# Stores moved from ScalarE's queue to GpSimd's queue with the one-packet option, and middle tiles computed in two rows

## The chip, the cores and the metric

The kernel runs on one core of a Trainium2 chip. The metric is the device time of one execution in microseconds, as the median of several runs. The span of a profile is about 1.4 us shorter than the device time of the same execution, so spans are compared with spans and times with times.

## The reference

```python
# x: 8192 x 8192 float32
def reference(x):
    a, b = np.split(x, 2, axis=-1)
    return a * (1 / (1 + np.exp(-b)))
```

It is a gated linear unit: the left half of each row times the sigmoid of the right half. 268.44 MB are read and 134.22 MB are written.

## The kernel before

The 8192 rows are cut into 32 tiles of 256 rows. A partition holds two neighbouring rows of x, so a load moves 128 pieces of 64 KB and a store 128 pieces of 32 KB. I call such a piece a "row" of the transfer; the records of the profile show one packet for each. Each of the 16 DMA engines has 8 rows of each transfer. There are two input slots and two output slots.

```python
    for i in range(n_tiles):
        # ... (bookkeeping of waits)
        load = nc.sync.dma_start(out=xs[i % SLOTS], in_=x_t[i])
        # ...
        if 0 < i < n_tiles - 1:
            parts = [(slice(0, R), slice(0, half))]
        else:                      # first and last tile: four quarters
            w = half // 2
            parts = [
                (slice(r, r + 1), slice(c * w, (c + 1) * w)) for r in range(R) for c in range(2)
            ]
        def store(cols):
            ins = nc.scalar.dma_start(out=out_t[i, :, cols], in_=os[i % SLOTS][:, cols])
            now["stores"].append(ins)

        for k, (r, c) in enumerate(parts):
            b = rows[:, r, 1, c]
            sig = nc.scalar.activation(out=b, in_=b, func=SIG)
            mul = nc.vector.tensor_mul(out=packed[:, r, c], in0=rows[:, r, 0, c], in1=b)
            # ... (which waits are kept: on odd tiles the sigmoid, else the product,
            #      waits for the store of two tiles before)
            if i == n_tiles - 1 and k > 0:
                store(chunks[k - 1])          # the last tile is stored in quarters
        store(chunks[-1] if i == n_tiles - 1 else slice(0, R * half))
```

## Time and profile before

| | before |
|---|---|
| time, median of 3 runs | 933.28 us (933.08 to 933.77) |
| span of the profile | 931.7 us |
| bytes, mean rate | 402.67 MB, 432 GB/s |
| VectorE (DVE), ScalarE (ACT), GpSimd (POOL) busy | 30%, 24%, 0% |
| period of a tile, (885.93 - 73.65) / 28 from the starts of the sigmoids of tiles 2 and 30 | 29.01 us |

The table says to look at the DMA engines and at nothing else: the compute engines idle most of the time, and the rate hardly leaves room. The prediction shows the lines. Two more carry the argument, the issues of the page (what, queue, how many, KB each, median us from issue to landing):

```profile
out_dram<-o_sb ACTq DMA_DIRECT2D x31, 4096.0 KB, 34.7
...
x_sb<-in_x_dram SPq DMA_DIRECT2D x32, 42.2
```

A store of 4 MB would take 9.7 us alone at 434 GB/s. It takes 34.7 us because it shares the engines with a load.

### The profile page before, as it was taken

Reading aid. Unit: us, or ns where it says so; the run is one execution under the profiler, and the core shown is the slowest. Engines: PE = TensorE matmul, PEld = TensorE weight load, DVE = VectorE, ACT = ScalarE, POOL = GpSimd, SP = SyncE. Lnnn points to the kernel's source line nnn. Section 1 sums busy time; section 2 is a strip of 40 time slices with the busy share of each in tenths; the row PEclk is TensorE's granted clock in tenths of the full one; section 3 lists DMA queues with packets and bytes.
Section 4 is the critical chain, followed back from the end, with each engine's and each line's share of the span. In section 5 each row is a group of like instructions: output and inputs, shape, how many; then the busy total and the mean of one; then the engine's idle time right before and its main releaser. Section 6 shows DMA issues by size and latency. Waiting matters only on the chain.

```text
span 931.7 us, 247 instructions
## 1 busy us (share of the span) xinstructions
DVE 278.7 (30%) x38; ACT 227.1 (24%) x39; POOL 0.2 (0%) x4
## 2 busy tenths in 40 slices
DVE  0333213333133331233312333123331233312333
ACT  1323330233311333113331133311333113332033
POOL 0000000000000000000000000000000000000000
DMA  9999999999999999999999999999999999999999
GB/s 405 428 450 428 422 456 405 450 428 428 450 418 438 428 436 442 428 428 450 447 408 428 442 459 428 413 460 411 450 428 425 453 408 447 428 428 450 425 430 405
DMA packets 9649, 402.67 MB, mean 432 GB/s; under 512 B 1072, under 2 KB 1072, under 8 KB 1072
## 3 DMA queue, kind: packets, MB, share of 16 engines
q1 hardware_dynamic: 4608, 268.44, 66.6%
q10 hardware_dynamic: 5040, 134.22, 33.4%
q14 instruction: 1, 0.01, 0.0%
HBM read 268.44 MB, written 134.22 MB: 432 GB/s over the span
## 4 chain that ended last, share of the span: by engine, by line
DMA 73%; DVE 15%; ACT 12%; issue 0%; ACTq 0%
DMA x_sb<-in_x_dram 73%; DVE o_sb L69 15%; ACT x_sb L68 12%; ACTq L62 0%; ACTq L68 0%
## 5 line engine op out<-in xcount | busy, mean ns | idle before, releaser
L69 DVE TENSOR_TENSOR o_sb<-x_sb 128x8192 f32<-128x8192 f32 (+1 forms) x38 | 278.7, 7344 | 647.1 <-ACT x_sb L68 647.1
L68 ACT ACTIVATE x_sb<-x_sb 128x8192 f32<-128x8192 f32 (+1 forms) x38 | 225.8, 5952 | 695.6 <-DMA x_sb<-in_x_dram 694.4
L68 ACT ACT_TABLE_LOAD x1 | 1.3, 1283 | 0.8 <-PEq L188 0.8
L188 POOL MEMSET const-bfloat16-1.0<- 128x1 bf16 x1 | 0.1, 102 | 0.0
L188 POOL MEMSET const-uint8-127<- 128x1 uint8 x1 | 0.1, 102 | 0.0
L188 POOL MEMSET const-float32-0.0<- 128x1 f32 x1 | 0.1, 99 | 0.2 <-issue 0.2
L188 POOL MEMSET const-float32-1.0<- 128x1 f32 x1 | 0.1, 99 | 0.0
## 6 DMA issues: line engine op xcount, KB each, us to landing
out_dram<-o_sb ACTq DMA_DIRECT2D x31, 4096.0 KB, 34.7
out_dram<-o_sb ACTq DMA_DIRECT2D x4, 1024.0 KB, 5.6
x_sb<-in_x_dram SPq DMA_DIRECT2D x32, 42.2
```

The costliest lines, as they stand in the source:

```text
L68: sig = nc.scalar.activation(out=b, in_=b, func=SIG)
L69: mul = nc.vector.tensor_mul(out=packed[:, r, c], in0=rows[:, r, 0, c], in1=b)
L188: nc = _bacc.Bacc("TRN2", target_bir_lowering=False, num_devices=1)
```

## The change

The intent is to take the stores off ScalarE's queue, to give each store to the DMA engines as one packet, so that it goes through in one piece, and to end a tile's product earlier by computing it in two rows (the two rows of x that a partition holds, not rows of a transfer).

```diff
         if 0 < i < n_tiles - 1:
-            parts = [(slice(0, R), slice(0, half))]
+            parts = [(slice(r, r + 1), slice(0, half)) for r in range(R)]
         ...
         def store(cols):
-            ins = nc.scalar.dma_start(out=out_t[i, :, cols], in_=os[i % SLOTS][:, cols])
+            to, of = out_t[i, :, cols], os[i % SLOTS][:, cols]
+            if i < n_tiles - 1:
+                ins = nc.gpsimd.dma_start(out=to, in_=of, single_packet=True)
+            else:
+                ins = nc.scalar.dma_start(out=to, in_=of)
             now["stores"].append(ins)
         ...
-            by_sigmoid = i % 2 == 1 and len(parts) == 1
-            implied(mul, *(s for s in old["stores"] if by_sigmoid or s not in freed))
-            if by_sigmoid:
-                for s in freed:
-                    tc.add_manual_dep(sig.ins, s.ins.name, DEP, reason="frees the output slot")
+            implied(mul, *(s for s in old["stores"] if k > 0 or s not in freed))
```

More of the change, by code (lines that the diff above doesn't have):

```diff
@@ L20, in _tiles @@
     P = nc.NUM_PARTITIONS
-    DEP = mybir.DependencyInfo(mybir.DependencyClass.Sync, mybir.DependencyReason.DATA)
     fp32 = mybir.dt.float32
```

## The prediction

> **What bounds the kernel now.** I read the page of the slowest core first, its engine shares, then its DMA rows and queues, then a table of stretches, then the waits of the load queue, and last the order of events at the end.
>
> ```profile
> span 931.7 us, 247 instructions
> DVE 278.7 (30%) x38; ACT 227.1 (24%) x39; POOL 0.2 (0%) x4
> ...
> DMA packets 9649, 402.67 MB, mean 432 GB/s; under 512 B 1072, under 2 KB 1072, under 8 KB 1072
> ...
> q1 hardware_dynamic: 4608, 268.44, 66.6%
> q10 hardware_dynamic: 5040, 134.22, 33.4%
> ```
>
> The busiest compute engine works 30% of the span. The 16 DMA engines are busy for 66.6 + 33.4 = 100% of it. 402.67 MB is no more than one read of x (8192 x 8192 x 4 = 268.44 MB) and one write of the result (134.22 MB). So no bytes can be saved, and the change saves none.
>
> The table of stretches says that this holds in each stage (columns: stretch, its length, busy time of DVE, ACT and POOL, clock, DMA share, GB/s):
>
> ```profile
> 100.00:158.00 58.00, 17.39 (x2) 14.06 (x2) 0.00 (x0) 1.00 1.00 434
> 842.00:900.00 58.00, 17.41 (x3) 14.06 (x2) 0.00 (x0) 1.00 1.00 434
> 914.00:918.00 4.00, 1.35 (x1) 3.29 (x2) 0.00 (x0) 1.00 1.01 434
> 918.00:922.00 4.00, 3.84 (x3) 2.77 (x3) 0.00 (x0) 1.00 0.86 371
> 922.00:926.00 4.00, 3.80 (x2) 1.48 (x1) 0.00 (x0) 1.00 1.01 426
> ```
>
> Two tiles (25.17 MB) take 58.0 us, that is 29.0 us a tile at 434 GB/s, and it is 434 with loads and stores mixed as well as with stores alone (914 to 918, after the last load). The one weak stretch is 918 to 922: 0.14 of 4 us, about 0.5 us. From the list of issues, a load takes 42.2 us from issue to landing and a store of 4 MB takes 34.7 us, both longer than the 29.0 us period, so each queue always has a transfer waiting behind the running one. The chain that ended last reads "DMA 73%; DVE 15%; ACT 12%", which looks as if 27% of compute could be gained. That is a trap: the chain follows one slot of two, and while it stands on ACT and DVE the DMA engines move the other slot's bytes. The load queue's own waits (859.9 us for the product, 30 times) are of the same kind: time in which the earlier load is still running.
>
> The end of the timeline (start, duration, engine, what):
>
> ```profile
> 885.93 7.03 ACT L68 ACTIVATE x_sb<-x_sb 128x8192 f32<-128x8192 f32 x1 [22.00 <-DMA x_sb<-in_x_dram]
> 892.99 8.69 DVE L69 TENSOR_TENSOR o_sb<-x_sb 128x8192 f32<-128x8192 f32 x1 [20.34 <-ACT x_sb L68]
> 901.72 0.34 ACTq L62 DMA_DIRECT2D out_dram<-o_sb  x1
> 914.71 3.71 ACT L68 ACTIVATE x_sb<-x_sb 128x2048 f32<-128x2048 f32 x2 [21.75 <-DMA x_sb<-in_x_dram]
> 916.65 4.49 DVE L69 TENSOR_TENSOR o_sb<-x_sb 128x2048 f32<-128x2048 f32 x2 [14.97 <-ACT x_sb L68]
> 918.98 0.34 ACTq L62 DMA_DIRECT2D out_dram<-o_sb  x1
> ```
>
> The last load lands at 914.7, and the first quarter of the last tile is issued as a store only at 919.0. Yet the DMA moves 434 GB/s between: the store of tile 30, issued at 901.7, is still being served. The old stores fill the hole in which the last tile is computed.
>
> **What the Trainium skill says.** "DMA: Bandwidth & Descriptors", section "Where 436 GB/s comes from", gives the ceiling as 16 ports x 32 B x 850 MHz = 435.2 GB/s. The trace agrees: 434 in the steady stages. An estimate from that page's figure: 402.65 MB cannot take under 925.2 us, 0.7% below the span. A gain of 2% would need 914.6 us and is excluded as long as the ceiling holds.
>
> The same page, section "Queues, rings and completion order", says that each DMA engine goes round its queues packet by packet and changes only between packets. The trace agrees: load 1 runs alone until the first store is issued at 32.82. With data from about 21.3, and some 1.6 us from issue to data (below), it has run 13.1 us of the 19.3 us that 8.39 MB take at 434 GB/s. Its other 6.2 us of work end near 44.2 (its sigmoid starts at 44.80), that is in 9.8 us, a share of 63%. Load rows here are 64 KB (268.44 MB / 4096 data packets), store rows 32 KB; turns of one row each give the load 2/3.
>
> The same page's "Specifications" give first byte about 1 us for GpSimd's path and 0.6 us for the other; no record of the kernel before shows GpSimd's path. "SBUF — State Buffer", section "Who interferes with whom", says that a product with two SBUF inputs takes GpSimd's read interface and not its write interface; the trace has no GpSimd work to check this.
>
> **The change, part by part.**
>
> Two rows. From the rows by shape: sigmoid 128x2048 1.903 us, 128x8192 7.031 us, so 128x4096 is about 3.61 us by a straight line; product 2.288 and 8.692 us, so about 4.42 us. The chain from landing to the end of the product goes from 7.03 + 8.69 = 15.7 us to 3.61 + 2 x 4.42 = 12.5 us. It frees the slot 3.2 us sooner, 30 times, 97 us if these lay on the path. But the next load is issued behind one that still has 29.0 - 12.5 = 16.5 us to run, where it had 13.2. Value in the steady state: 0. Busy time rises by 30 x (0.19 + 0.15) = 10 us on two engines that idle 70%: 0.
>
> The waits. Products wait for the store of two tiles before; it landed 34.7 us after an issue that lies 58 us back, so this wait was and stays empty: 0.
>
> The queue. 31 issues of 0.36 us leave ACT, off the path: 0. GpSimd, idle until now, builds the descriptors; I allow 2 us from the product to the first byte, and no queue runs dry by it: 0.
>
> The one-packet option. I take it, as an assumption, that each DMA engine's share of a store (8 rows of 32 KB, 256 KB) then is one turn. At 434/16 = 27.1 GB/s the turn takes 9.7 us, in which the load stands still; between two load rows (2.4 us each) the whole store goes by. The sum over a period stays 19.3 + 9.7 = 29.0 us, so the steady state stays. But a store lands 2 + up to 2.4 + 9.7 + about 1 = 13 to 15 us after issue, and a load takes 58.0 - 12.5 = 45.5 us. And at the end the order changes. Store 30 is issued 12.5 us after load 30 lands, starts by 12.5 + 2 + 2.4 = 16.9 and is out by 26.6 us, while load 31 ends at 29. So store 30 is wholly served ahead of load 31, and nothing is left to fill the hole.
>
> How large is this? In the kernel before, stores got 1/3 of 433.9 GB/s from about 34.4 to 914.1: 127.2 MB. The first 31 stores are 130.0 MB. So 2.8 MB, 6.5 us, were left behind the last load. A second way: in the window 918 to 922 the 32 KB packets end at about 920.4, and 920.4 - 914.1 = 6.3 us. These come before load 31 now: it lands at 914.7 + 6.4 = 921.1. From there the tail is not shorter. The first quarter's store is issued 918.98 - 914.71 = 4.27 us after landing and its 8 KB packets began near 920.7, 1.7 us later; its data starts 6.0 us after landing as before, four quarters need 4.19 MB / 434 = 9.7 us, and the rest is completion. Landing to end was 931.7 - 914.7 = 17.0 us and stays 16.7 to 17. Sum: 0 + 0 + 0 + 6.4 - 0.2 = +6.2 us, so 933.3 + 6.2 = 939.5 us.
>
> **The rivals.**
>
> A. The option does not make one turn of a store (the packet is cut, or a store waits for the load row after next and slips past the end of load 31). For it: there is no packet of that size in the trace, and the margin for store 30 is 29 - 26.6 = about 2.4 us. Against: the name. Then the turns are as before, some stores are left behind the last load, and the time is 933 to 934.5 us.
>
> B. GpSimd's path costs DMA rate: descriptors are fetched from memory, engines leave step, or the change between a long write turn and reads costs something each time. For it: nothing before shows this queue. Against: only 9 descriptors a tile and engine, and pure stretches of loads and of stores ran at 426 to 434 GB/s. 1% is 9 us: 942 to 950.
>
> C. The earlier product or the end of turn-taking lifts the rate, as reads and writes no longer mix. For it: 434 to 435.2 is open. Against: that is 0.3%, 2.5 us; with the tail lost or kept, 931 to 937.
>
> **Range and chances.** I give 0.65 to the full loss of the filler (938 to 940.5), 0.2 to A, 0.1 to B, 0.05 to C. The middle of this is near 938.5; 8 in 10 lie between 932.5 and 942. Faster by over 2% needs the ceiling broken: 0.01. Slower by over 2% needs 18.7 us, B at double strength: 0.03. Within 2%: 0.96.
>
> **What would show it.** Right: stores land in 13 to 15 us instead of 34.7 and loads in about 45.5; the period stays 29.0 us and the share of DMA 1.00 in the middle; the last load lands near 921; then a stretch of about 6 us with hardly any bytes; landing to end about 17 us. Wrong: stores still near 35 us and a last landing near 914.7 (A); a period over 29.2 us (B) or under 28.95 (C); or a hole of 6 us somewhere in the middle, which would mean that a load was issued too late.

## The result, and the profile after

The changed kernel takes 933.91 us (median of 4 runs, 933.23 to 934.19); the kernel before took 933.24 us beside it. The ratio is 1.0005 with a 95% interval of 0.9991 to 1.0019, so no difference is seen. A ratio is the mean time of one kernel's runs over that of the other's of the same rounds, so it is not quite the ratio of the medians quoted. Executions over 1.5% slower than the fastest of the same kernel are left out of the means.

The page of the changed kernel:

```profile
span 931.9 us, 316 instructions
DVE 280.8 (30%) x68; ACT 229.8 (25%) x69; POOL 16.8 (2%) x35
...
q1 hardware_dynamic: 4608, 268.44, 66.6%
q0 software_dynamic: 4464, 130.03, 32.3%
q10 hardware_dynamic: 576, 4.19, 1.1%
...
out_dram<-o_sb POOLq DMA_DIRECT2D x31, 4096.0 KB, 37.9
...
x_sb<-in_x_dram SPq DMA_DIRECT2D x32, 45.5
```

(q1 carries the loads, q0 the stores that GpSimd issues, q10 those that ScalarE issues.) The move did happen: 130.03 MB now go by the software queue q0. But its 4464 records are 31 x 144, that is 128 rows and 16 semaphore writes a store, as on the old queue. And a store does not land in 13 to 15 us, as the prediction has it. It lands in 37.9 us. That is 34.7 + 3.2 us: the product ends 3.2 us earlier, the store is issued 3.2 us earlier, and it lands when it did before. The load shows the same shift, from 42.2 to 45.5 us.

Two tiles in the middle and the stretches at the end (the same columns as in the prediction):

```profile
842.00:900.00 58.00, 17.52 (x4) 14.24 (x4) 1.06 (x2) 1.00 1.00 434
914.00:918.00 4.00, 1.20 (x1) 3.14 (x2) 0.00 (x0) 1.00 0.95 410
918.00:922.00 4.00, 3.81 (x3) 2.48 (x2) 0.00 (x0) 1.00 0.88 377
922.00:926.00 4.00, 3.68 (x2) 1.91 (x1) 0.00 (x0) 1.00 1.01 428
```

The 6 us without bytes that the prediction expected near the end are not there. The end of the timeline:

```profile
885.92 7.12 ACT L71 ACTIVATE x_sb<-x_sb 128x4096 f32<-128x4096 f32 x2 [21.72 <-DMA x_sb<-in_x_dram]
889.57 8.76 DVE L72 TENSOR_TENSOR o_sb<-x_sb 128x4096 f32<-128x4096 f32 x2 [20.08 <-ACT x_sb L71]
898.62 0.53 POOL L63 DMA_DIRECT2D out_dram<-o_sb  x1 [28.30 <-DVE o_sb L72]
914.86 3.71 ACT L71 ACTIVATE x_sb<-x_sb 128x2048 f32<-128x2048 f32 x2 [21.82 <-DMA x_sb<-in_x_dram]
```

Sigmoid, product and issue of tile 30 come as predicted, 12.7 us after the landing at 885.92. The last load lands at 914.86 us, not at 921, and the bytes of earlier stores that are still to move after it are the same: counted from some 0.6 us before the last tile's sigmoid, when the data of load 31 are through, to the end, the queues of stores move 6.88 MB before (from 914.1 us) and 6.84 MB after (from 914.3 us: 4.19 on q10 and 2.65 on q0). Less the 4.19 MB of the last tile this is 2.69 and 2.65 MB. I call it the filler. The prediction needed it to be zero.

Rows that began in a stretch with both queues at work, 48 to 52 us, in the changed kernel (queue, records, MB, share; a row counts whole where it begins):

```profile
q1 hardware_dynamic: 16, 1.05, 60.5%
q0 software_dynamic: 16, 0.52, 30.3%
```

Sixteen load rows and sixteen store rows: on each engine one of the one, then one of the other, with the option on. The kernel before has the same two counts in the same stretch.

### The profile page after: what moved, and what is told of

Read it like the earlier page. It is cut to its first block, busy times and chain, and to the rows that moved or that the text cites. A ratio compares the mean times of both kernels' runs of the same rounds, so it can differ in the third digit from the quotient of the medians.

```text
span 931.9 us, 316 instructions
## 1 busy us (share of the span) xinstructions
DVE 280.8 (30%) x68; ACT 229.8 (25%) x69; POOL 16.8 (2%) x35
## 3 DMA queue, kind: packets, MB, share of 16 engines
q0 software_dynamic: 4464, 130.03, 32.3%
q10 hardware_dynamic: 576, 4.19, 1.1%
## 4 chain that ended last, share of the span: by engine, by line
DMA 78%; DVE 15%; ACT 6%; issue 0%; ACTq 0%
DMA x_sb<-in_x_dram 78%; DVE o_sb L72 15%; ACT x_sb L71 6%; ACTq L65 0%
## 5 line engine op out<-in xcount | busy, mean ns | idle before, releaser
L72 DVE TENSOR_TENSOR o_sb<-x_sb 128x4096 f32<-128x4096 f32 (+1 forms) x68 | 280.8, 4171 | 645.6 <-ACT x_sb L71 645.6
L71 ACT ACTIVATE x_sb<-x_sb 128x4096 f32<-128x4096 f32 (+1 forms) x68 | 228.5, 3407 | 693.5 <-DMA x_sb<-in_x_dram 691.8
L63 POOL DMA_DIRECT2D out_dram<-o_sb x31 | 16.6, 536 | 882.1 <-DVE o_sb L72 882.1
## 6 DMA issues: line engine op xcount, KB each, us to landing
out_dram<-o_sb POOLq DMA_DIRECT2D x31, 4096.0 KB, 37.9
x_sb<-in_x_dram SPq DMA_DIRECT2D x32, 45.5
```

Of the source, the lines that this page charges most:

```text
L63: ins = nc.gpsimd.dma_start(out=to, in_=of, single_packet=True)
```

## The experiments

Theory T: a turn is one row, whatever the option says, so stores are served as before; the prediction's account of the end is right and its condition was not met. Rivals: the option acts and something else made up for it (R); the option acts on shorter rows (R2) or on smaller stores only (R3); or the order at the end costs nothing in any case.

### Without the option

```diff
-                ins = nc.gpsimd.dma_start(out=to, in_=of, single_packet=True)
+                ins = nc.gpsimd.dma_start(out=to, in_=of)
```

> The changed kernel without the one-packet option. Theory T (turns between the queues are taken row by row, and the option does not lengthen a store's turn here): nothing moves, stores land in 37.9 us as with the option (within 0.5 us), last load lands at 914 to 915.5, time within 0.15% of the changed kernel's 933.9 us. Rival R (the option does act, and something else made up for it): store landing moves by more than 3 us, and the time by more than 2 us.

Measured: 933.61 us beside 933.15 us for the kernel before, ratio 1.0001 (0.9986 to 1.0015). The issues of its page:

```profile
out_dram<-o_sb POOLq DMA_DIRECT2D x31, 4096.0 KB, 37.8
...
x_sb<-in_x_dram SPq DMA_DIRECT2D x32, 45.5
```

Last load at 915.13 us, filler 2.69 MB. Nothing moves. R falls: the option had no effect at this shape. Whether it is dropped on the way to the chip, or reaches the chip and changes nothing, no run here tells.

### Store rows of 8 KB, with and without the option

```diff
-  nc.gpsimd.dma_start(out=to, in_=of, single_packet=True)
+  nc.gpsimd.dma_start(out=to, in_=of, single_packet=True, max_dma_last_dim=8192)   # first kernel
+  nc.gpsimd.dma_start(out=to, in_=of, max_dma_last_dim=8192)                       # second kernel
```

> The changed kernel with store rows cut from 32 KB to 8 KB (32 rows for each DMA engine and store), the option kept. T: a turn is one row of 8 KB against a load row of 64 KB, stores get 1/9 while loads run, so a store lands only in 45 to 56 us, loads land early and then wait, time 932 to 940. Rival R2 (the option works, but 32 KB rows were too long for it): a store is one turn of 256 KB, lands in 13 to 16 us, the last load lands near 921, time 938 to 941.

> As the run with 8 KB store rows, without the option. T: equal to that run in all (store landing within 1 us, time within 0.15%). R2: this one has store landings of 45 to 56 us and that one 13 to 16 us, so they differ widely.

Measured: 973.62 us with and 973.68 us without, beside 933.15 us. (`max_dma_last_dim` cuts the rows of a transfer to this many bytes.) Stores land in 51.5 and 51.6 us, loads in 31.9 and 31.8 us. Rows that began from 40 to 44 us in the kernel with the option:

```profile
q1 hardware_dynamic: 32, 1.05, 60.7%
q0 software_dynamic: 32, 0.26, 15.4%
```

16 of the 32 load records are the semaphore writes that end load 1 (1.05 MB are 16 rows of 64 KB); the 32 of q0 are rows of 8 KB. Counting the semaphore writes, it is still one to one, now with 8 KB against 64 KB. So R2 falls: turns did not get longer with the option, and the two kernels are equal. The landings were forecast; the time was not (932 to 940). I had thought that the engines would stay busy with stores while loads wait. The waits of the kernel with the option show what is new (engine, line, for what: us in total, times, longest):

```profile
DVE o_sb L72 <- DMA out_dram<-o_sb: 641.5, 30, 42.6
```

Stores now get so small a share that the products of 30 of the 32 tiles wait for one. Sigmoids start 22.6 and about 38.1 us apart in turn, 60.7 us for two tiles in place of 58.0; 15 such pairs are 40 us, the whole loss. The records of the trace say where some 2.7 us a pair are lost, if each row's bytes are spread over its own time: from 402 to 407 us, after both loads have landed and the old store ends, 1.46 MB move where the full rate would move 2.17, so 1.6 us are lost in this one gap. Another 0.5 us go from 445 to 449 us, and the 8 KB rows alone run at 428 GB/s.

### Load rows of 8 KB

```diff
-        load = nc.sync.dma_start(out=xs[i % SLOTS], in_=x_t[i])
+        load = nc.sync.dma_start(out=xs[i % SLOTS], in_=x_t[i], max_dma_last_dim=8192)
```

> The changed kernel with load rows cut from 64 KB to 8 KB. T, with the prediction's account of the end: turns of 32 KB against 8 KB give the store 4/5, it lands in 14 to 16 us (9.7 x 5/4 + 3), store 30 is out before load 31, the last load lands near 921, then some 6 us nearly without bytes, time 939 to 940.5. Rival (the order of stores and loads at the end costs nothing, or the hole is hidden by something else): stores land early and the time stays at 933 to 935. If 8 KB rows cost DMA rate, the period in the middle shows it: over 29.1 us.

Measured: 955.34 us beside 933.15 us. The issues:

```profile
x_sb<-in_x_dram SPq DMA_DIRECT2D x32, 8192.0 KB, 46.6
out_dram<-o_sb POOLq DMA_DIRECT2D x31, 4096.0 KB, 16.7
```

Here a store does go through nearly in one piece, by turns of 32 KB against 8 KB (43 store rows and 45 load rows began from 40 to 44 us). It lands in 16.7 us, a little over the range given, no filler is left (0.00 MB after the last load's data), and some 6 us pass nearly without bytes at the end (2 GB/s from 936 to 940 us, 131 from 940 to 944). But the time that I forecast, 939 to 940.5 us, was missed: the short rows also cost rate all along, which I had only allowed for. From 882 to 895 us, with loads alone, they run at 422 GB/s in place of 434, and the period is (908.29 - 81.66) / 28 = 29.52 us, 0.51 us over 29.01, or 16 us for 31 periods. Of the 22 us some 6 are left for the end. The two are not separated by this run, so the last run below was made.

### Load rows of 32 KB

```diff
+        load = nc.sync.dma_start(out=xs[i % SLOTS], in_=x_t[i], max_dma_last_dim=32768)
```

> The changed kernel with load rows of 32 KB, as long as the store rows. T: the store gets 1/2 while both run; it starts about 14.5 us after its load landed, has 13.9 us until the next load is done, so 6.9 of its 9.7 us are served, 2.7 us are left as filler against 6.4 before. Store landing about 22 us, last load at 918 to 919, time 936 to 938, between the changed kernel and the 8 KB load rows. Rival (the step is all or nothing, or not of the tail): 933 to 934.5, or over 939.

Measured: 939.56 us (938.06 to 944.93), beside 934.22 us; ratio 1.0067 (1.0037 to 1.0097). Stores land in 23.6 us, the last load at 922.62 us, and only 0.10 MB of filler are left, not the 1.2 MB (2.7 us) that I expected. The loss is more than the half that I expected, and the time lies in the range that I gave to the rival (over 939). But the turns are those of theory T. Rows that began from 42 to 50 us:

```profile
q0 software_dynamic: 64, 2.10, 60.6%
q1 hardware_dynamic: 63, 1.54, 44.7%
```

16 of the 63 load records are semaphore writes, which take a turn each, so it is one to one again. What differs is that the engines no longer end their shares together. The 16 semaphore writes that end load 31 begin between 917.6 and 922.2 us, 14 of them before 919, where I had put the landing; in the changed kernel all 16 begin between 913.6 and 914.4 us. A load has landed only when its last engine is done, and the engines that were done earlier went on with their store rows: 2.10 MB of stores begin from 917.6 us on, 2.03 of them before 922.3. So there was filler, but it was moved while the last engine still loaded. Why the engines drift apart here, and why the tiles came 25.6 and 32.7 us apart in turn over much of the run, I did not find out.

### Two rows alone, and the queue alone

```diff
-                ins = nc.gpsimd.dma_start(out=to, in_=of, single_packet=True)   # rows alone
+                ins = nc.scalar.dma_start(out=to, in_=of)

-            parts = [(slice(r, r + 1), slice(0, half)) for r in range(R)]       # queue alone
+            parts = [(slice(0, R), slice(0, half))]
```

> Two rows of middle tiles alone, stores on the ACT queue as before. T: products end 3.2 us sooner, store and load landings grow by 3.2 us (37.9 and 45.4), the time stays: 932.9 to 934. Rival (ending sooner is worth something, or delays the sigmoid on ACT behind the store's issue): under 932 or over 935.

> The queue of GpSimd alone, with whole-tile sigmoid and product. T: stores land in 34.7 us (within 0.7), loads in 42.2, time 933 to 934.3. Rival (GpSimd's path costs rate and the two rows win it back): period over 29.05 us, time over 935.

Measured: rows alone 934.32 us, queue alone 933.78 us, beside 934.22 us; ratios 1.0000 (0.9983 to 1.0017) and 0.9997 (0.9982 to 1.0012). Both medians are in noise of the kernel before; the first is 0.3 us over the range that I gave, but the kernel before was 1 us slower in these rounds too. Stores land in 38.2 and 34.5 us, loads in 45.5 and 42.2 us: the 3.2 us come from the rows alone, and GpSimd's path lands a store no later than ScalarE's. The periods are 29.01 and 29.02 us. So neither part gave something that the other took back.

### 8 KB load rows in all loads but the last

```diff
+        load = nc.sync.dma_start(out=xs[i % SLOTS], in_=x_t[i],
+                                 max_dma_last_dim=8192 if i < n_tiles - 1 else 65536)
```

> 8 KB load rows in all loads but the last, which keeps 64 KB rows. T: stores 2 to 29 land early (14 to 16 us), but store 30 shares with the 64 KB rows of load 31: 1/3 of 13.9 us = 4.6 us are served before that load is done and 5 us are left as filler. So nearly all of the loss of the run with 8 KB rows everywhere comes back: time 934 to 936, 4 to 5.5 us under it. Rival (8 KB load rows cost time all along the run): the time stays within 1.5 us of the run with 8 KB rows in all loads.

Measured: 948.56 us beside 934.22 us, 6.8 us under the 955.34 us of 8 KB rows in all loads (that from an earlier call, whose kernel before was 1.1 us faster). The filler is back: 3.18 MB. The absolute range was missed, since I left the lost rate of 16 us out of it; the difference, forecast as 4 to 5.5 us, came out somewhat larger, as more filler was left than the 2.2 MB (5 us) expected. One load of 32 decides some 7 us, so the rival (the cost lies all along the run) explains only the rest.

### Stores in four parts of 32 partitions, with and without the option

```diff
-                ins = nc.gpsimd.dma_start(out=to, in_=of, single_packet=True)
+                for q in range(0, P, 32):
+                    now["stores"].append(nc.gpsimd.dma_start(
+                        out=to[q : q + 32], in_=of[q : q + 32], single_packet=True))   # without it in the second
...
-            implied(mul, *(s for s in old["stores"] if k > 0 or s not in freed))
+            implied(mul, *(s for s in old["stores"] if s not in freed))
```

The second edit keeps the waits of each row's product.

> Each store of a middle tile as four stores of 32 partitions (32 rows of 32 KB in all, 2 for each DMA engine), with the option; the product of each row keeps its waits. Asks whether the option did nothing only because a store of 128 rows was too much for one packet. T (turns are single rows whatever the option says): store and load rows go by one to one while both run, the same rows, landings and time as the same kernel without the option (landing within 1 us, time within 0.2%). Rival R3 (a small enough store is one turn): two store rows to each load row, the last of the four stores of a tile lands in about 22 to 28 us after issue instead of some 38, and the time is 3 to 7 us over the kernel without the option. Splitting by partitions may itself cost DMA rate; that would hit both alike.

> The four stores of 32 partitions without the option: the other half of the pair. T: as with the option. R3: store rows one to one with load rows here, two to one there. If the split itself costs nothing, the time is 933 to 935 here.

Measured: 1033.43 us (1027.96 to 1038.99) with, 1028.41 us (1024.31 to 1034.01) without, beside 933.31 us; a fourth run without, 1044.82 us, is slow and left out. Rows that began from 48 to 52 us with the option:

```profile
q1 hardware_dynamic: 16, 1.05, 60.5%
q0 software_dynamic: 16, 0.52, 30.3%
```

The same two lines hold for the kernel without it: one to one, with two rows for each engine in a store. Landings are 39.6 and 39.2 us for each part, where R3 had 22 to 28. The times do not decide: their difference is within the 3 to 7 us of R3 and over the 0.2% of T, but the runs of each kernel lie 10 us apart. So R3 falls by rows and landings, as far as these shapes reach. The split itself costs some 100 us, and I had allowed for no such size; the engines' mean rate falls to 392 GB/s, and the products wait 663 us for stores. That cost was not taken apart further; in this run the engines end their shares of a load 6.3 us apart (median), in the changed kernel 0.5 us.

### More filler: 8 KB rows in the store of tile 30 alone

```diff
-   single_packet=True)
+   single_packet=True, max_dma_last_dim=8192 if i == n_tiles - 2 else 65536)
```

> The changed kernel with 8 KB rows in the store of tile 30 alone, so that it gets 1/9 beside load 31 and more of it is left behind that load. T: load 31 lands about 2 us sooner (912 to 913.5), the filler grows from 2.65 MB to 3.5 to 4 MB and closes the gap of some 0.5 us before the first store of the last tile; the end moves by that alone: 0.3 to 0.6 us faster, 933.2 to 933.7, which may lie in the noise. Rival (more filler means a later end, since the last tile's stores queue behind it): slower by 1 us or more.

Measured: 933.53 us (5 runs) beside 933.31 us, ratio 1.0004 (0.9992 to 1.0017). The start of the last tile in its timeline:

```profile
913.22 3.71 ACT L71 ACTIVATE x_sb<-x_sb 128x2048 f32<-128x2048 f32 x2 [19.90 <-DMA x_sb<-in_x_dram]
```

The last load lands 1.6 us earlier and the filler is 3.72 MB, counted as before from 912.6 us, both as expected; the end does not move beyond noise. The last tile's stores land in 7.6 us instead of 5.5, as they now queue behind the filler. The hole was full already (see the section on a faster version), so more filler is worth nothing.

### 8 KB rows in the load of tile 31 alone

```diff
+        load = nc.sync.dma_start(out=xs[i % SLOTS], in_=x_t[i],
+                                 max_dma_last_dim=8192 if i == n_tiles - 1 else 65536)
```

> The changed kernel with 8 KB rows in the load of tile 31 alone, all other transfers as they were: the order at the end by itself, without the cost of 8 KB rows along the run. T with the prediction's account of the end: store 30 gets 4/5 beside load 31, is out before it, the bytes of earlier stores left behind the last load fall from 2.65 MB to under 0.2 MB, load 31 lands 6 to 7.5 us later (920.9 to 922.4), then some 5 us with hardly any bytes, time 939 to 941, that is 5.5 to 7 us over the changed kernel. Rival (the filler is worth less than its bytes): under 937.

Measured: 940.21 us (940.01 to 940.29) beside 933.25 us, ratio 1.0074 (1.0057 to 1.0091). Its stretches at the end:

```profile
922.00:926.00 4.00, 1.03 (x1) 2.98 (x2) 0.00 (x0) 1.00 0.01 4
926.00:930.00 4.00, 3.81 (x3) 2.77 (x3) 0.00 (x0) 1.00 0.47 197
930.00:934.00 4.00, 4.00 (x2) 1.79 (x1) 0.00 (x0) 1.00 1.03 426
```

And its timeline from the last load on:

```profile
923.02 3.71 ACT L71 ACTIVATE x_sb<-x_sb 128x2048 f32<-128x2048 f32 x2 [29.55 <-DMA x_sb<-in_x_dram]
924.97 4.49 DVE L72 TENSOR_TENSOR o_sb<-x_sb 128x2048 f32<-128x2048 f32 x2 [26.20 <-ACT x_sb L71]
927.29 0.37 ACTq L65 DMA_DIRECT2D out_dram<-o_sb  x1
```

This is the end that the prediction described, brought about on purpose: after the last load the DMA engines move 4 GB/s for 4 us and half of their rate for the next 4, until the first quarter of the last tile is stored. No filler is left on q0. The load lands at 923.02 us, 0.6 us later than the range I gave and 8.2 us later than in the changed kernel; 2.65 MB at 434 GB/s are 6.1 us of this, the cost of 8 KB rows some 0.5 us (the 0.51 us of a period above). Some of the other 1.5 us is that the engines end their shares of this load apart from each other: from 921 to 923 us only 0.20 MB move, where 0.43 MB a microsecond is the full rate. The rest I cannot place. From there to the end it takes 938.9 - 923.0 = 15.9 us, 1.1 us less than the 17.0 us of the changed kernel, as the quarters land in 4.2 us with nothing ahead of them. The sum is 8.2 - 1.1 = 7 us, as measured.

### A faster version?

None was found. The bytes alone take 402.65 MB / 433.9 GB/s = 928.0 us at the rate of the middle, and the span is 931.7 us. Where the other 3.7 us go can be worked out from the records of the kernel before, each row's bytes spread over its own time: 1.9 us are lost in the first 5 us, 0.9 from 36 to 40 us, when the first store's rows come in, and 0.7 after 930 us. There is no gap before the last tile's stores: 1.73 MB move from 914 to 918 us and 1.73 from 918 to 922. The 371 GB/s of that stretch in the table come from counting each row whole where it begins. So the run with more filler had nothing to close.

## Why the prediction was wrong

**The bound** was right. The period stayed at 29.0 us and 434 GB/s in the changed kernel, in each part alone and without the option.

**Two rows, waits and queue** were each put at zero and are zero: rows alone 1.0000, queue alone 0.9997. The sizes inside held too: row operations of 3.61 and 4.42 us by a straight line measured 3.608 and 4.422 us, the load landing of 45.5 us was met, and the two tiles in the middle took the same 17.52 us of VectorE with stores on GpSimd and on ScalarE, so no contention with GpSimd is seen. GpSimd is busy 0.53 us for an issue.

**The one-packet option** is the step that failed: "I take it, as an assumption, that each DMA engine's share of a store (8 rows of 32 KB, 256 KB) then is one turn." A turn was one row with the option and without it: landing 37.9 and 37.8 us, 16 rows to 16. It was so for 8 rows of 32 KB, 32 rows of 8 KB and 2 rows of 32 KB an engine. The landing of 13 to 15 us, the last load at 921 us and the sum of +6.2 us all hung on it. Rival A had this case with its number (933 to 934.5 us), at a chance of 0.2 against 0.65. "Against: the name" was the whole argument against it, and that was too little for such a weight. Why the option made no difference stays open.

**The account of the end** was right, but its condition was never met. The filler was put at 2.8 MB from the shares and 6.3 us from the window; it measures 2.69 MB. When the order is forced by short rows in the last load, the time is 940.2 us against the predicted 939.5. The tail was put at 16.7 to 17 us and took 15.9: the first quarter's store began 0.9 us after its issue (928.17 and 927.29 us), where the prediction had 1.7 us, read where filler was still ahead of it. The load came later than put by about 2 us. The two partly cancel, so that 940.2 is so near to 939.5 is in part luck.

**Two readings** in the prediction do not hold. The weak stretch from 918 to 922 us, "about 0.5 us", is no gap, as told above. And the share of 63% was reckoned with store data 1.6 us after the first issue at 32.82 us; the first store row begins at 38.81 us, 6.0 us after it. That one-row turns came out of this sum was luck; the counts of rows show them.

**Rivals B and C** are not seen: periods from 29.01 to 29.02 us with either queue.

## What to carry to other kernels

In this kernel, whose DMA engines are full from start to end, moving an issue, ending a product sooner or splitting it was worth nothing. What still counts is the end: some bytes that need no computing should be left to move while the last tile is computed. Which transfer goes first was set here by the lengths of their contiguous rows, not by the option named for it; count the rows that begin on each queue in a stretch before trusting such an option.

## What the Trainium skill lacked or had wrong

- "DMA: Bandwidth & Descriptors", section "Queues, rings and completion order", gives a turn as a packet of typically about 9 to 17 descriptors. Here it was one row in the stretches counted: 16 load rows of 64 KB to 16 store rows of 32 KB, 16 rows plus 16 semaphore writes to 32 rows of 8 KB, and with equal rows of 32 KB 64 store records to 63 load records.
- No page says what the one-packet option does to a plain store. Here nothing changed with it: landings of 37.9 and 37.8 us, 51.5 and 51.6 us, 39.6 and 39.2 us, with and without.
- "DMA: Bandwidth & Descriptors", section "Specifications", gives 512 B as the least transfer for line rate. Here loads alone ran at 422 GB/s with rows of 8 KB and at 434 with rows of 64 KB, and a tile took 29.52 us in place of 29.01, 1.8% more.
- No page gives how far apart the 16 engines end one transfer. Here it was 0.8 us for the last load of the changed kernel, and 4.6 us with load rows of 32 KB, where the load landed that much later than its first share.
